# Splitting three of sixteen input tiles into 16 KiB row halves in a DMA-bound interleave

## The chip, the cores and the metric

One core of one Trainium2 chip. The metric is the device time of one execution in microseconds (us). In this document "before" and "after" are the two kernels, "x2" is the second x tile, "store 3" the third of the sixteen output stores, and "row" one partition's contiguous piece of a transfer, 32 KiB if nothing else is said.

## The reference

```python
batch, seq, dim = 32, 256, 1024          # x, y: float32, 33.55 MB each
result = np.zeros((batch, seq, dim * 2), dtype=np.float32)
result[..., 0::2] = x
result[..., 1::2] = y
```

Nothing is computed. 67.11 MB are read, 67.12 MB written.

## The kernel before: the parts that matter

Eight pairs of x and y tiles of 128 x 8192 elements (4 MiB) are loaded on one DMA queue (SP). Each pair gives two output tiles: VectorE (DVE) copies half of x to the even and half of y to the odd columns, and a second queue (ACT) stores 128 x 8192 elements. Each of these three pools has two buffers. A store of 8 KiB of zeros goes ahead of all others on the ACT queue, in both kernels; it explains the 0.01 MB more that are written.

```python
xpool = ctx.enter_context(tc.tile_pool(name="xp", bufs=2))   # yp, op: bufs=2 too
# ... cut ...
    nc.sync.dma_start(out=xtile, in_=xs)       # [128 x 8192], rows of 32 KiB
    nc.sync.dma_start(out=ytile, in_=ys)
    soff = 0
    while soff < lw:                           # two output tiles per pair
        # ... cut: otile and os_ ...
        nc.vector.tensor_copy(out=otile[:, 0::2], in_=xsub)
        nc.vector.tensor_copy(out=otile[:, 1::2], in_=ysub)
        nc.scalar.dma_start(out=os_, in_=otile)
        soff += width
```

So the two queues depend on each other: a store waits for an x and a y tile, a copy waits for the store two before it (its output buffer), a load waits for the copies of the pair two before it. Code that follows the loop moves the first load ahead of a barrier and shortens the end; the change leaves it alone.

## Time and profile before

| | before |
|---|---|
| median time, first measurement | 315.43 us (315.37 to 315.51) |
| span of the profiled run | 313.6 us |
| DVE busy | 72.8 us, 23% |

The lines of the page that carry this are in the prediction. One more view is needed later: the windows around the moment when the first store joins the loads, and one from the middle of the kernel to compare with. The columns are the stretch, its length, DVE busy time and count, POOL the same, clock, DMA share, and GB/s.

```profile
22.00:26.00 4.00, 4.00 (x2) 0.00 (x0) 1.00 0.95 410
26.00:30.00 4.00, 0.44 (x1) 0.00 (x0) 1.00 1.03 377
30.00:34.00 4.00, 0.00 (x0) 0.00 (x0) 1.00 1.02 442
...
182.00:186.00 4.00, 2.36 (x2) 0.00 (x0) 1.00 0.91 393
```

Read the last two columns together. A window of 4 us holds only some three rows of each engine, so GB/s alone swings, to 393 even in the middle of the kernel, but there the DMA share falls with it. GB/s divided by the share tells what the engines move while they are busy: 432, 366, 433 and 432 in these four windows. So there is a dent from 26 to 30 us, where the stores start: packets are in flight all along, at a share of 1.03, but last longer.

### The profile page before, as it was taken

Reading aid. Unit: us, or ns where it says so; the run is one execution under the profiler, and the core shown is the slowest. Engines: PE = TensorE matmul, PEld = TensorE weight load, DVE = VectorE, ACT = ScalarE, POOL = GpSimd, SP = SyncE. Lnnn points to the kernel's source line nnn. Section 1 sums busy time; section 2 is a strip of 40 time slices with the busy share of each in tenths; the row PEclk is TensorE's granted clock in tenths of the full one; section 3 lists DMA queues with packets and bytes.
Section 4 is the critical chain, followed back from the end, with each engine's and each line's share of the span. In section 5 each row is a group of like instructions: output and inputs, shape, how many; then the busy total and the mean of one; then the engine's idle time right before and its main releaser. Section 6 shows DMA issues by size and latency. Waiting matters only on the chain.

```text
span 313.6 us, 140 instructions
## 1 busy us (share of the span) xinstructions
DVE 72.8 (23%) x33; POOL 0.2 (0%) x4
## 2 busy tenths in 40 slices
DVE  0433002231022410325003150131501305023500
POOL 0000000000000000000000000000000000000000
DMA  8999999999999999999999999999999999999997
GB/s 344 460 405 397 464 405 464 405 464 405 460 410 447 422 439 431 435 435 426 443 410 460 401 468 401 468 401 464 405 464 405 464 405 460 410 447 422 439 431 334
DMA packets 4640, 134.23 MB, mean 428 GB/s; under 512 B 528, under 2 KB 544, under 8 KB 544
## 3 DMA queue, kind: packets, MB, share of 16 engines
q1 hardware_dynamic: 2304, 67.11, 50.0%
q10 hardware_dynamic: 2336, 67.12, 49.6%
HBM read 67.11 MB, written 67.12 MB: 428 GB/s over the span
## 4 chain that ended last, share of the span: by engine, by line
DMA 83%; DVE 11%; DVEq 1%; issue 0%
DMA out_dram<-otile 76%; DMA ytile<-in_y_dram 7%; DVE otile L72 6%; DVE otile L71 5%; DVEq L84 1%; DVEq L71 0%
## 5 line engine op out<-in xcount | busy, mean ns | idle before, releaser
L71 DVE COPY otile<-xtile 128x4096 f32<-128x4096 f32 x16 | 36.6, 2295 | 184.8 <-DMA out_dram<-otile 173.6
L72 DVE COPY otile<-ytile 128x4096 f32<-128x4096 f32 x16 | 36.6, 2292 | 39.8 <-DMA ytile<-in_y_dram 39.8
L46 DVE MEMSET zero<- 16x128 f32 x1 | 0.2, 165 | 0.9 <-PEq L134 0.9
L134 POOL MEMSET const-bfloat16-1.0<- 128x1 bf16 x1 | 0.1, 101 | 0.0
L134 POOL MEMSET const-uint8-127<- 128x1 uint8 x1 | 0.1, 101 | 0.0
L134 POOL MEMSET const-float32-0.0<- 128x1 f32 x1 | 0.1, 98 | 0.2 <-issue 0.2
L134 POOL MEMSET const-float32-1.0<- 128x1 f32 x1 | 0.1, 98 | 0.0
## 6 DMA issues: line engine op xcount, KB each, us to landing
out_dram<-otile ACTq DMA_DIRECT2D x16, 4096.0 KB, 29.1
xtile<-in_x_dram SPq DMA_DIRECT2D x8, 4096.0 KB, 43.6
ytile<-in_y_dram SPq DMA_DIRECT2D x8, 4096.0 KB, 60.7
out_dram<-zero ACTq DMA_DIRECT2D x1, 8.0 KB, 6.3
```

What stands on the lines that cost most here:

```text
L46: nc.vector.memset(zero, 0.0)
L71: nc.vector.tensor_copy(out=otile[:, 0::2], in_=xsub)
L72: nc.vector.tensor_copy(out=otile[:, 1::2], in_=ysub)
L84: tc.compile()
L134: nc = _bacc.Bacc("TRN2", target_bir_lowering=False, num_devices=1)
```

## The change

x2, y2 and y8 are loaded as two column halves, with rows of 16 KiB, so that copies can wait for half a tile and the stores get more of the engines beside those loads.

```diff
-        nc.sync.dma_start(out=xtile, in_=xs)
-        nc.sync.dma_start(out=ytile, in_=ys)
+        for t, s, parts in (
+            (xtile, xs, 2 if start == P * lw else 1),
+            (ytile, ys, 2 if start in (P * lw, total - P * lw) else 1),
+        ):
+            step = lw // parts
+            for c in range(0, lw, step):
+                nc.sync.dma_start(
+                    out=t[:, c : c + step],
+                    in_=dataclasses.replace(s, offset=start + c, ap=[[lw, P], [1, step]]),
+                )
```

## The prediction

> **What bounds the kernel now.** I read the page first: busy shares, the forty slices, the DMA queues. The columns of the slices are tenths of busy time, one digit per 7.84 us.
>
> ```profile
> DVE 72.8 (23%) x33; POOL 0.2 (0%) x4
> DMA  8999999999999999999999999999999999999997
> q1 hardware_dynamic: 2304, 67.11, 50.0%
> q10 hardware_dynamic: 2336, 67.12, 49.6%
> HBM read 67.11 MB, written 67.12 MB: 428 GB/s over the span
> ```
>
> The only compute engine with work, DVE, is busy 23%. The DMA engines are busy in every slice, and their two queues (q1 loads, q10 stores) fill 99.6% of 16 engines' span between them. A 4 MiB load has 128 rows; 16 loads of 128 rows plus 16 completion entries make 16 x 144 = 2304, the count of q1. So one packet is one 32 KiB row, and each of the 16 engines moves 8 rows of every tile.
>
> Second, the chain of waits. Read alone it misleads, and that is the trap here:
>
> ```profile
> by line: DMA out_dram<-otile 76.4%; DMA ytile<-in_y_dram 6.7%; DVE otile L72 5.7%; DVE otile L71 5.1%; DVEq L84 0.7%; issue 0.2%; DVEq L71 0.0%
> ```
>
> It says that the end waits on stores for 76% of the time, as if faster stores would shorten it. But a store takes long only because loads run beside it. Third, the queues' view of the stretch from 72 to 111 us shows this (columns: packets, MB, share):
>
> ```profile
> q1 hardware_dynamic: 288, 8.39, 49.8%
> q10 hardware_dynamic: 288, 8.39, 49.8%
> ```
>
> Equal packets and equal bytes: the engines serve the queues one row each in turn. Fourth, the timeline (start, length, instruction, idle before it and what ended it):
>
> ```profile
> 12.23 4.50 DVE L71 COPY otile<-xtile 128x4096 f32<-128x4096 f32 x2 [11.20 <-DMA xtile<-in_x_dram]
> 21.95 4.50 DVE L72 COPY otile<-ytile 128x4096 f32<-128x4096 f32 x2 [5.22 <-DMA ytile<-in_y_dram]
> 48.10 2.29 DVE L71 COPY otile<-xtile 128x4096 f32<-128x4096 f32 x1 [21.66 <-DMA out_dram<-otile]
> 55.31 2.29 DVE L72 COPY otile<-ytile 128x4096 f32<-128x4096 f32 x1 [4.92 <-DMA ytile<-in_y_dram]
> 67.47 2.29 DVE L71 COPY otile<-xtile 128x4096 f32<-128x4096 f32 x1 [9.87 <-DMA out_dram<-otile]
> 94.03 2.30 DVE L72 COPY otile<-ytile 128x4096 f32<-128x4096 f32 x1 [4.96 <-DMA ytile<-in_y_dram]
> 132.76 2.29 DVE L72 COPY otile<-ytile 128x4096 f32<-128x4096 f32 x1 [4.92 <-DMA ytile<-in_y_dram]
> 287.66 2.30 DVE L72 COPY otile<-ytile 128x4096 f32<-128x4096 f32 x1 [4.92 <-DMA ytile<-in_y_dram]
> 293.79 2.30 DVE L71 COPY otile<-xtile 128x4096 f32<-128x4096 f32 x1 [3.83 <-DMA out_dram<-otile]
> ```
>
> Loads alone: x1 lands at 12.23, y1 at 21.95, so 9.72 us for 8 rows, 1.215 us a row. With both queues: y3 lands at 94.03, y4 at 132.76, so 38.73 us for 32 rows an engine, 1.21 us a row or 2.42 us for a load row and a store row. The two rates agree to 0.4%. One queue with work fills the engines; a second only divides them. The whole work is 256 rows an engine, 256 x 1.21 = 309.8 us of a span of 313.6. Of the other 3.8 us, some 2.5 are the start (12.23 - 9.72); what is left is the last landing and the end of the program. **The bound is total DMA work, not stores.**
>
> **What the Trainium skill says.** "DMA: Bandwidth & Descriptors", section "Queues, rings and completion order": each DMA engine round-robins between the queue rows that have work, at packet granularity. The 288 against 288 packets above agrees. The same page, "Where 436 GB/s comes from": a ceiling of 435.2 GB/s, set by 16 ports. The trace's steady period moves 16.78 MB in 38.73 us, 433 GB/s, so it stands within 0.5% of it. The same page, "Why small descriptors are slow (HBM only)": a fixed overhead of about 3 cycles a packet; no run here isolates it yet. "SBUF — State Buffer", "The DMA setup-cost knee": a roughly fixed 2 us a transfer, mostly completion latency; the 2.5 us of x1 is of that kind, and behind a queued transfer it is hidden, since y1 came 9.72 us after x1.
>
> **The change part by part.** No byte is added or removed. The loads of x2, y2 and y8 become two each, of 16 KiB rows, so q1 gets 3 x 144 = 432 more packets. DVE and ACT keep their instructions in order. The built order shows that the copies wait on halves separately: the third pair of copies needs x2's and y2's first halves only, and the very last y copy alone needs y8's second half. It also shows one new wait in the load queue: y2's second half waits for x1's semaphore. That is over at 12.23 us, while y1 still loads, so it costs nothing.
>
> *Share.* Where 16 KiB load rows meet 32 KiB store rows in turn, a store row comes every 1.5 x 1.21 = 1.82 us in place of 2.42, and stores get two thirds of the engines. I carry this through. In before, x2 and y2 (16 rows) land 33.36 us after y1; n rows at 1.215 and 16 - n at 2.42 give n = 4.46 rows alone, then sharing from 27.4 us. Store 1 landed at 48.10, so in landing terms it began 8 x 2.42 earlier, at 28.7, which is 4.5 us after its issue.
> - Store 1 lands at 28.7 + 8 x 1.82 = 43.3 (48.10 before), store 2 at 57.8 (67.47).
> - Loads: 3.54 rows of x2 are left, 7.1 halves, then 8 halves of y2's first part: 27.4 + 15.1 x 1.82 = 54.8. After a copy of 2.29 store 3 is issued at 57.1 and begins, with the same 4.5 us, at 61.5. **So stores starve for 3.7 us.** Loads run alone then, y2's second half lands at about 62, and the engines stay full.
> - x3 starts at 62, not 55.3, and lands at about 81.3; store 3 lands at 80.3 (86.77 before), so the copy after it waits for x3. Store 4 ends at 99.7; y3 lands at 99.5 (94.03), store 5 begins at 101.8 + 4.5 = 106.3, a store gap of 6.6 us. In it x4 gets 4.5 rows alone, just as x2 did at the start, then 3.5 rows at 2.42 and y4's 8 give y4 at 132.9 against 132.76 before.
>
> The head start of the stores is thus handed back in full by about 125 us, with the engines busy all along: gain 0.
>
> *End.* x8 lands at 287.66 - 8 x 2.42 = 268.3. y8's first half takes 8 x 1.82, to 282.8, the second to 297.3 (whole y8 before: 287.66). Store 14 lands at about 292 (293.79 before). The last y copy ends at 297.3 + 2.3 = 299.6, and store 16 is issued then, against 298.3 before. Store 15 holds the engines till about 303.4 in landing terms (293.79 + 8 x 1.21), since the bytes ahead of it are the same. Store 16's entry needs 2.5 us (x1's, alone) to 4.5 us (store 1's, shared): ready at 302.1 to 304.1. The chance of a bubble is real, its size at most 0.7 us; near the lower figure there is none.
>
> *Packets.* 24 more rows an engine. Estimate from the skill's 27.2 GB/s an engine (435.2 / 16): a 32 KiB row would take 1.205 us, the trace has 1.210, so at most 0.006 us a row is overhead of any kind: 24 x 0.006 = 0.14 us, and three more completion entries of like size, 0.02 us.
>
> Sum: 315.43 + 0.16 + 0 for the shares + a bubble of 0 to 0.7 that I weight down to 0.05 = 315.6.
>
> **The rivals.**
> 1. *Stores are the bound, as the chain says.* Then 9.6 us earlier for store 2 would carry to the end: about 306 us. Against it: the DMA slices show no room, and 306 less the launch would ask for 134.23 MB in some 304 us, 441 GB/s, over every steady rate seen here. I give it almost nothing.
> 2. *A starved store queue becomes idle engines.* Loads fall 7 us behind, and with two buffers a tile each load waits on copies. If both queues ran dry in the two store gaps, up to 3.7 + 6.6 = 10.3 us would be lost: 326. Against it: x3 and y3 are issued at 16.75 and 26.5, long before they are needed, and by my count x4 at 60 and y4 at 64, ahead of the second gap.
> 3. *Half rows cost more per byte.* They are 12 MiB of 128, about 29 us of DMA time; 5% worse would be 1.5 us, 317. Nothing in the trace has 16 KiB rows, so this is not excluded.
> 4. *The bubble ahead of store 16*: up to 0.7 us, 316.3.
> 5. *Turns go by bytes, not packets*: no shift at all, 315.5. The trace before cannot tell, all rows being equal.
>
> **Range and chances.** 315.6, with 0.7 us below for a boundary or a start that I misplaced, and 1.0 above for rivals 3 and 4 in part: 314.9 to 316.6. Two per cent is 6.3 us, more than the 3.8 us not spent on rows, so faster has 0.01; slower needs rival 2, 0.02; within 2% 0.97.
>
> **What would show it.** Right: loads x19, q1 with 2736 packets; the third x copy starts near 43.3 and the fourth near 57.8; a new DVE wait for x3 ends near 81; y4 lands within 1 us of 132.8; the DMA row of the slices stays at 9; the last y copy starts near 297. With turns by bytes the third x copy stays near 48. Wrong: a slice with DMA at 7 or less in the middle, a y4 several us late, or a gap in DMA between the last two stores of over 1 us.

## The result, and the profile after

| | before | after |
|---|---|---|
| median | 315.47 us | 318.01 us |
| lowest to highest of 6 runs | 315.35 to 315.84 | 316.45 to 323.67 |
| ratio of the fast runs | | 1.006, interval 1.0035 to 1.0084 |

A ratio is the mean time of one kernel's fast runs over that of the other's in the same rounds, so it is not quite the ratio of the two medians. Two of the six runs of after (322.80 and 323.67) count as slow, being over 1.5% above the fastest run of their kernel, and are left out of it; no clock below 1.00 is on record for them, and no run of before was so far above its fastest. The change is a small loss, and it makes the time scatter: the four fast runs alone cover 1.9 us, where six of before cover 0.5.

The page of after, the lines that answer to those of the prediction:

```profile
DMA  9999999999999999999999999999999999999996
...
q1 hardware_dynamic: 2736, 67.11, 49.9%
q10 hardware_dynamic: 2336, 67.12, 49.3%
HBM read 67.11 MB, written 67.12 MB: 425 GB/s over the span
```

And the chain of waits of after, its shares by line:

```profile
by line: DMA out_dram<-otile 63.5%; another core or an unknown queue 11.9%; DMA ytile<-in_y_dram 6.8%; DVE otile L82 6.5%; DVE otile L81 5.8%; issue 0.9%; DVEq L81 0.1%
```

The 2736 packets are as counted, the DMA row still says 9, and the chain hangs on stores for 63.5% of the time where it was 76.4%. (Its "unknown queue" pieces, 11.9%, stand in the timeline of after at the waits for y2, x3, y3 and y8.) The page does not show where two microseconds went: they are lost inside slices that read "busy". The queues' view from 30 to 54 us of after, while half rows meet whole store rows:

```profile
q10 hardware_dynamic: 230, 7.01, 67.6%
q1 hardware_dynamic: 231, 3.28, 31.9%
```

Equal packets, twice the bytes for stores: turns go by rows, as predicted. The timeline of after:

```profile
45.12 2.29 DVE L81 COPY otile<-xtile 128x4096 f32<-128x4096 f32 x1 [18.41 <-DMA out_dram<-otile]
54.89 2.30 DVE L82 COPY otile<-ytile 128x4096 f32<-128x4096 f32 x1 [7.48 <-DMA ytile<-in_y_dram]
59.69 2.29 DVE L81 COPY otile<-xtile 128x4096 f32<-128x4096 f32 x1 [2.51 <-DMA out_dram<-otile]
...
64.63 2.29 DVE L82 COPY otile<-ytile 128x4096 f32<-128x4096 f32 x1 [2.64 <-DMA ytile<-in_y_dram]
...
84.02 2.29 DVE L81 COPY otile<-xtile 128x4096 f32<-128x4096 f32 x1 [17.09 <-DMA xtile<-in_x_dram]
...
133.95 2.30 DVE L82 COPY otile<-ytile 128x4096 f32<-128x4096 f32 x1 [4.37 <-DMA ytile<-in_y_dram]
...
299.35 2.29 DVE L82 COPY otile<-ytile 128x4096 f32<-128x4096 f32 x1 [3.12 <-DMA ytile<-in_y_dram]
```

Every event of the predicted ledger is there, in order, and each is 0.1 to 2.7 us late against it (43.3, 54.8, 57.8, 62, 81.3, 132.9, 297.3). The new wait for x3 ends at 84. The windows at the start of the stores, as above, now for after:

```profile
22.00:26.00 4.00, 3.79 (x2) 0.00 (x0) 1.00 1.00 430
26.00:30.00 4.00, 0.71 (x1) 0.00 (x0) 1.00 1.10 344
30.00:34.00 4.00, 0.00 (x0) 0.00 (x0) 1.00 0.98 422
```

The dent is deeper: GB/s over share is 430, 313 and 431, where before had 366 in the middle window.

**Looking at the sixteen engines one by one.** A transfer is complete when each of 16 DMA engines has set its mark. The Trainium skill says so in "DMA: Bandwidth & Descriptors", section "Why a DMA increments its semaphore by 16 and not by 1": the engines "finish independently, and the semaphore counts them". The trace has a time for each mark. First, middle (median) and last of the 16, worked out from those records:

```
                       before                      after
                       first   middle  last        first   middle  last
y1                     21.41   21.64   21.92       21.33   21.65   22.19
store 1                47.57   47.67   47.97       42.99   44.02   44.99
y2 (after: 2nd half)   54.84   54.97   55.29       61.20   62.83   64.61
x3                     74.21   74.34   74.65       80.88   82.20   83.94
y4                    132.29  132.42  132.74      131.49  133.08  133.92
y8 (after: 2nd half)  287.19  287.31  287.63      296.12  297.70  299.33
store 16              312.60  312.72  313.04      313.05  313.67  315.03
```

In before the sixteen marks of a transfer lie within 0.5 us for the whole kernel. In after they spread to 3.4 us and stay apart. Every wait is for the last of them. The end is later by 1.99 us (313.04 to 315.03). Of this the mean of the marks gives 0.99 (312.75 to 313.74), and the lag of the last behind the mean gives 1.00 (0.29 to 1.29). The other 0.26 of the 2.25 us by which the spans differ lies behind the last landing; I did not look into it.

The packets can be sorted into 16 chains, since on a busy engine one starts as the one before ends; each chain then holds 256 rows' worth of bytes, with a few packets put down to the wrong one in some of the runs. An engine's delay is its time less 1.2105 us for each row done. That gives a ledger for every run, shown after the experiments.

### The profile page after: what moved, and what is told of

It is laid out like the page before. It is cut to its first block, busy times and chain, and to the rows that moved or that the text cites. A ratio compares the mean times of both kernels' runs of the same rounds, so it can differ in the third digit from the quotient of the medians.

```text
span 315.8 us, 144 instructions
## 1 busy us (share of the span) xinstructions
DVE 72.9 (23%) x33; POOL 0.2 (0%) x4
## 3 DMA queue, kind: packets, MB, share of 16 engines
q1 hardware_dynamic: 2736, 67.11, 49.9%
## 4 chain that ended last, share of the span: by engine, by line
DMA 70%; DVE 12%; another core or an unknown queue 12%; issue 1%; DVEq 0%
DMA out_dram<-otile 63%; DMA ytile<-in_y_dram 7%; DVE otile L82 6%; DVE otile L81 6%; DVEq L81 0%
```

## The experiments

Thirteen runs were made, in four calls, before and after themselves among them; each call was on one chip (4, 6, 7 and 7), with before beside it. The first theories: A, the loss arises where stores first start beside half rows of x2; B, the shifted share costs in itself; C, each half row costs alike. After the first call came D: where the stores outrun the loads, restarts set the engines apart; against P: half rows cost by themselves. The edits of the loads are given as the two lines that choose `parts`, and all edits are written here more shortly than in the runs (there, for one, `start // (P * lw) in (1,)`), to the same effect. The intervals beside the ratios are 95%.

### First call: one part at a time

Only x2 halved:

```diff
-            (ytile, ys, 2 if start in (P * lw, total - P * lw) else 1),
+            (ytile, ys, 1),
```

> Only the second x tile is loaded in two halves. Theory A (the loss comes where stores first start beside 16 KiB load rows, near 26 us): nearly the whole loss, ratio 1.004 to 1.008, the 16 landings of the last store 1.5 to 2.5 us apart (0.45 before), and times that scatter by several us as in the changed kernel. Theory B (the loss comes from the shifted share and the starving store queue): about half the shift, so a ratio of 1.002 to 1.004. Theory C (every half row costs alike): a third of the loss, ratio 1.002, no scatter.

316.21 us (316.07 to 316.31), ratio 1.0015 (1.0003 to 1.0027). The delay at the start of the stores is there, 1.21 us against 0.66, but not the whole loss, and the times do not scatter. The last marks are only 0.18 us apart: store 15 was issued so late that the engines sat idle for 0.28 us on average, and all left that wait together. Theory A in its strong form is out.

Only y2 halved:

```diff
-            (xtile, xs, 2 if start == P * lw else 1),
-            (ytile, ys, 2 if start in (P * lw, total - P * lw) else 1),
+            (xtile, xs, 1),
+            (ytile, ys, 2 if start == P * lw else 1),
```

> Only the second y tile is loaded in two halves; stores now start beside 32 KiB rows of x2. Theory A: no loss, ratio 1.000 to 1.001, landings of the last store about 0.5 us apart, no scatter. Theory B: stores still get two thirds during y2, ratio 1.002 to 1.004. Theory C: ratio 1.002.

316.67 us (315.73 to 317.67), ratio 1.0032 (1.0015 to 1.0048). Here A expected nothing, while B's range holds it. In the profiled run the mean of the last marks is only 0.22 us later than before's; one engine is 0.85 us behind that mean.

Only y8 halved:

```diff
-            (xtile, xs, 2 if start == P * lw else 1),
-            (ytile, ys, 2 if start in (P * lw, total - P * lw) else 1),
+            (xtile, xs, 1),
+            (ytile, ys, 2 if start == total - P * lw else 1),
```

> Only the last y tile is loaded in two halves, far from the start of the stores. Theory A: ratio within 1.000 to 1.001, spread of the last landings about 0.5 us. Theory C: ratio 1.002. If a bubble ahead of the last store were the cause (the bubble of the prediction): ratio 1.002 to 1.005 and an idle stretch between the last two stores.

316.19 us (315.33 to 317.20), ratio 1.0016 (1.0002 to 1.0029). In the profiled run nearly all of the loss was in place at 32 us, 195 us before y8 is even issued: 0.92 us of delay at the start of the stores, three engines 2 us late in their stores. So this profile cannot charge the loss to y8's halves, and no idle stretch lies between the last two stores. What the halves of y8 themselves cost is not separated. Until 226 us this run issues what before issues, so 0.92 against 0.66 also shows how much that start differs between executions.

x2 and y2 halved, y8 whole:

```diff
-            (ytile, ys, 2 if start in (P * lw, total - P * lw) else 1),
+            (ytile, ys, 2 if start == P * lw else 1),
```

> Second x and y tile in halves, last y whole. Theory A: as x2 alone, ratio 1.004 to 1.008, scatter of several us. Theory B: the same. Theory C: two thirds, 1.004. If the halves of the last y tile matter, this is clearly faster than the changed kernel (1.006).

316.70 us (316.19 to 318.43), ratio 1.0042 (1.0023 to 1.0061). Not to be told from after's 1.006, nor from the sum of its two parts. By size alone, the ratios of the parts (1.0015, 1.0032, 1.0016) add up to after's, as theory C wants it; but C has no such price in the trace, as the next calls show.

### Second call: chance, place and dose

Before, unchanged, as a control:

> The kernel before, unchanged, as a control: how far one profile of it differs from another. If stepping out of line at the start of the stores is only chance and happens in it too, its engines' last landings are sometimes 1 us apart and its mean delay at that start 0.6 to 0.9 us; time 315.4 to 316.0, ratio 1.000.

315.74 us (315.45 to 316.00), ratio 0.9996 (0.9984 to 1.0008), on chip 6. Delay at the start of the stores 0.68 us, last marks 0.49 us apart. The order of before is no accident of one profile.

After, unchanged:

> The changed kernel, unchanged, on another chip: ratio 1.005 to 1.010, again times that scatter by 2 us or more, last landings 1 us or more apart and a delay of 1.1 to 1.3 us at the start of the stores (near 26 us). If the scatter was a matter of the first chip, all times lie within 1 us.

317.77 us (316.02 to 333.04; the highest counts as slow), ratio 1.0054 (1.0016 to 1.0093). The loss and the scatter came again, here on chip 6. In its profile y8's second half spread over 4.6 us, its last mark came at 300.54, and store 16 could only be issued then. Its windows near there:

```profile
296.00:302.00 6.00, 2.85 (x2) 0.00 (x0) 1.00 1.00 431
302.00:306.00 4.00, 0.86 (x1) 0.00 (x0) 1.00 0.86 369
```

This is the bubble of the prediction's rival 4: 0.41 us of idle time an engine, in this run, none in the other profile of after. The slowest engine decides whether it opens.

The fourth pair halved in place of the second:

```diff
-            (xtile, xs, 2 if start == P * lw else 1),
-            (ytile, ys, 2 if start in (P * lw, total - P * lw) else 1),
+            (xtile, xs, 2 if start == 3 * P * lw else 1),
+            (ytile, ys, 2 if start == 3 * P * lw else 1),
```

> The same halves two tile pairs later, in the fourth x and y tile, when stores have long run. Theory A (the loss is at the first meeting of stores and half rows): no more than 1.001 to 1.002. Theory D (any stretch with halves lets the store queue starve, and engines that are out of line then lose time at each restart): 1.003 to 1.005 like the second tile.

318.27 us (316.14 to 319.15), ratio 1.0068 (1.0041 to 1.0094). Theory A allowed 1.002 at most. The loss does not need the first start of the stores. In the profile 37 rows after 32 us last over 5% longer than they should, 0.85 us an engine, most of them near 160 and 183 to 186 us, long after the halves. And y8, whole here, lands between 287.98 and 292.43 us, one engine 4 us after the middle. The timeline and the windows of this run:

```profile
292.45 2.29 DVE L82 COPY otile<-ytile 128x4096 f32<-128x4096 f32 x1 [6.91 <-DMA ytile<-in_y_dram]
294.78 7.46 ACTq L83 DMA_DIRECT2D out_dram<-otile  x2
```

```profile
290.00:294.00 4.00, 1.55 (x1) 0.00 (x0) 1.00 0.91 393
294.00:298.00 4.00, 1.38 (x2) 0.00 (x0) 1.00 0.67 287
```

No loads are left, store 14 is done on most engines, and store 15 waits for the slowest engine's y8: a share of 0.67. That is 1.46 us of idle time an engine. Here GB/s over share stays at 432 and 428: engines that idle lower both, rows that last longer lower the quotient.

The same trace has a restart that the argument has to take in. From about 177 us the store queue runs dry again, and it restarts near 184 us with whole rows alone on both queues:

```profile
182.00:186.00 4.00, 3.47 (x2) 0.00 (x0) 1.00 1.05 393
```

The quotient is 374. By the packets, the last load row ahead of the first store row lasted 1.2 to 2.1 times its length on 11 of the 16 engines. The marks of y5, which landed just before, were 2.3 us apart. So a restart can cost without half rows beside it, in this run where the engines were already out of step.

x2 in four quarters, all else whole:

```diff
-            (xtile, xs, 2 if start == P * lw else 1),
-            (ytile, ys, 2 if start in (P * lw, total - P * lw) else 1),
+            (xtile, xs, 4 if start == P * lw else 1),
+            (ytile, ys, 1),
```

> Second x tile in four quarters with 8 KiB rows, all else whole. Theory A, with a dose: the delay at the start of the stores grows over the 1.2 us of halves (0.7 with whole rows), to some 1.5 us; if the delay is set by a fixed time in which loads run at half speed, it stays at 1.2 us. Store 1 should land near 41, as stores get four fifths while x2 loads.

316.21 us (315.93 to 316.42), ratio 1.0010 (0.9997 to 1.0023). The delay at the start is 1.22 us, as with halves (1.21): not a dose per row. Store 1's middle mark is at 41.3, as expected. The engines are 5.4 us apart near 60 us and back within 0.62 at the end: being apart for a while does not cost the end by itself.

### Third call: shares against rows

All loads halved, all stores whole:

```diff
-            (xtile, xs, 2 if start == P * lw else 1),
-            (ytile, ys, 2 if start in (P * lw, total - P * lw) else 1),
+            (xtile, xs, 2),
+            (ytile, ys, 2),
```

> All loads in two halves, all stores whole: stores get two thirds in every tile pair, so the store queue runs dry and restarts again and again. Theory D (each restart beside unequal rows sets engines further apart and the 16 landings are waited for together): well above the changed kernel, ratio 1.010 or more, last y landings 4 us or more apart. Theory P (half rows cost by themselves): 240 more rows an engine at the 0.002 us that a half row showed, and the start of the stores once, ratio 1.003 to 1.005 and no scatter.

321.69 us (321.44 to 321.80), ratio 1.0185 (1.0171 to 1.0200). The largest loss. (The 240 in the expectation is a slip: 4608 packets on q1 in place of 2304 are 128 more rows an engine, which makes theory P's share smaller still.) Marks of one transfer are up to 8.85 us apart, 135 rows are stretched (2.50 us an engine) and the engines idle for 1.77 us. Its list of who waits for whom has turned over; the first two lines (total us, times, longest), and then the line of before for the wait for y:

```profile
DVE otile L82 <- DMA ytile<-in_y_dram: 118.3, 16, 16.3
DVE otile L81 <- DMA out_dram<-otile: 101.3, 7, 14.9
```

```profile
DVE otile L72 <- DMA ytile<-in_y_dram: 39.8, 8, 5.2
```

So the wait for y grew from 39.8 to 118.3 us: the stores now outrun the loads, and each store is started by the slowest engine's load.

All loads and all stores halved, which adds to the edit just shown:

```diff
-            nc.scalar.dma_start(out=os_, in_=otile)
+            for c in range(0, 2 * width, width):
+                nc.scalar.dma_start(
+                    out=dataclasses.replace(
+                        of, offset=2 * start + 2 * soff + c, ap=[[2 * lw, P], [1, width]]
+                    ),
+                    in_=otile[:, c : c + width],
+                )
```

> All loads and all stores in halves: twice the rows, but the two queues take equal turns and the store queue does not run dry. Theory D: ratio 1.002 to 1.006 (some 1 us of row cost, 0.5 us at the start of the stores), landings of one transfer within 1.2 us of each other, scatter under 1 us. Theory P: more than all loads in halves, as it has twice as many half rows.

317.16 us (317.15 to 317.21), ratio 1.0044 (1.0032 to 1.0056). Twice as many half rows as in the run before, and 64 transfers in place of 48, with a quarter of its loss: theory P is out, and so is the number of transfers. The marks of a transfer lie 0.3 us apart through the middle of the run, one row is stretched, and the five times cover 0.06 us. The price of a row can be read here: from 32 to 288 us the mean delay grows by 1.08 us while before's falls by 0.07; 256 us are 211 rows of 1.2105, each cut in two, so 1.15 / 211 = 0.005 us an extra row.

All rows whole, x3 loaded ahead of y2, so that store 3 comes late and its queue runs dry (the kernel before, cut to the core of the edit):

```diff
+            if start == P * lw:          # second pair: its y waits behind the next x
+                ahead = load_x(2)        # the third pair then uses `ahead`
             nc.sync.dma_start(out=ytile, in_=ys)
```

> All rows whole; the third x tile is loaded ahead of the second y tile, so that the third store comes late, the store queue runs dry near 67 us for some 7 us and restarts, as in the changed kernel, but without half rows. If a restart by itself costs: 0.3 us or more of delay near 73 us, ratio 1.002 or more, engines out of line after it. If it takes half rows to set the engines apart: ratio 1.000 to 1.001, landings after the restart within 0.6 us, or as far apart as they were before it.

315.56 us (315.33 to 316.30), ratio 0.9996 (0.9983 to 1.0009). The timeline of this run shows the late store:

```profile
67.56 2.29 DVE L81 COPY otile<-xtile 128x4096 f32<-128x4096 f32 x1 [17.07 <-DMA out_dram<-otile]
...
71.14 4.50 DVE L82 COPY otile<-ytile 128x4096 f32<-128x4096 f32 x2 [1.28 <-DMA ytile<-in_y_dram]
73.47 2.56 ACTq L83 DMA_DIRECT2D out_dram<-otile  x2
```

Store 2 has landed at 67.5 and store 3 is issued at 73.5. The engines go on with loads, the delay does not move (2.65 us at 32 and at 60, 2.64 at 110), and the last marks are 0.48 us apart. The windows around the restart, near 78 us, have no dent (GB/s over share 434 and 431):

```profile
74.00:78.00 4.00, 1.64 (x1) 0.00 (x0) 1.00 1.04 451
78.00:82.00 4.00, 0.00 (x0) 0.00 (x0) 1.00 0.93 401
```

The expected 0.6 us between marks was missed: from 84 us until the loads end they are 1.2 to 1.7 us apart, since three engines took one load row more ahead of their first store row. That changed the order of turns and cost nothing. So in this run, with marks 0.5 us apart when it came, a dry and restarted store queue was free; loads did fill it, as I had predicted. With the fourth pair halved, where the engines were out of step, it was not (above).

x2 and y2 halved with the two stores beside them halved too (stores of the first pair only, same store edit under `start == 0`):

> Second x and y tile in halves, and the two stores of the first tile, which run beside them, in halves too: equal turns, no starved store queue, first y halves still allow an early third store. Theory D: mean delay at the start of the stores of 0.7 to 1.2 us, then flat; ratio 1.001 to 1.003, under the second tile's halves alone (1.004), with less scatter (under 1 us). If half rows and not shares set the engines apart: as the second tile's halves alone, 1.004.

316.31 us (316.03 to 316.76), ratio 1.0014 (1.0001 to 1.0027), against 1.0042 for the same loads beside whole stores. The delay at the start is 0.83 us in place of 1.27. The intervals just overlap, and the profile is not clean: its engines were 3.4 us apart at worst and 32 rows were stretched, 0.45 us an engine, after the stores had gone back to whole rows. So this supports D in the time but not in the order of the engines that I expected.

### Fourth call: the mirror

All stores halved, all loads whole: the loads edit of the kernel before with the store edit shown above.

> The mirror of all loads in halves: all stores in halves, all loads whole, so loads get two thirds of the turns in bytes. If unequal rows on the two queues set the engines apart whichever side is short: later rows stretched by 1 us an engine or more, landings of one transfer 3 us or more apart, ratio 1.008 or more. If it takes stores that outrun the loads (a store queue that runs dry and restarts beside short load rows): some 128 x 2 more rows at 0.005 us, ratio 1.003 to 1.005, landings within 1.5 us, few stretched rows.

316.37 us (316.13 to 316.53), ratio 1.0016 (1.0004 to 1.0029). No row after 32 us is stretched, no engine idles, marks stay within 1.81 us. That is the second case, though the ratio lies below its range and the marks above its 1.5 us (the edit adds 128 rows an engine, not 128 x 2; at 0.005 us they are 0.64 us). The same inequality the other way round costs 0.16%, where halved loads beside whole stores cost 1.85%. So it is not inequality as such: it takes short load rows beside long store rows. Stores that get ahead of the loads came with that in every run, so the two are not separated.

### The ledger of all runs

Worked out from the packets and the marks of each profiled run, in us. "Start" is the growth of the mean delay from 24 to 32 us, where the stores first join (not given where they join before 24); "stretched" counts the rows after 32 us that last over 5% longer than 1.213, 0.611 or 0.308 us for their size, with the excess for each engine; "idle" adds gaps of over 0.1 us on an engine after 32 us; "mean" is how much later than before's the mean mark of the last store lands; "last" is how far its last mark is behind that mean; "apart" is the widest spread of a transfer's marks after 30 us.

```
kernel                       ratio   start  stretched    idle   mean   last   apart
before                               0.66     0  0.00    0.00   0.00   0.29   0.46
before again                 0.9996  0.68     0  0.00    0.00   0.04   0.34   0.53
x3 ahead of y2, whole rows   0.9996  0.67     1  0.01    0.00   0.08   0.30   1.73
x2 in quarters               1.0010  1.22     0  0.00    0.00   0.67   0.38   5.37
second pair and its stores   1.0014  0.83    32  0.45    0.00   0.79   0.58   3.38
x2 halves                    1.0015  1.21     0  0.00    0.28   0.93   0.09   2.87
y8 halves                    1.0016  0.92     2  0.02    0.00   0.29   0.65   2.22
all stores in halves         1.0016  0.58     0  0.00    0.00   0.83   0.36   1.81
y2 halves                    1.0032  0.81     1  0.02    0.00   0.22   0.85   2.25
x2 and y2 halves             1.0042  1.27     0  0.00    0.00   0.69   0.47   3.07
all loads and stores         1.0044  -        1  0.02    0.02   1.44   0.62   0.86
after again                  1.0054  0.99    35  0.49    0.41   1.43   2.09   4.62
after                        1.006   1.23    30  0.27    0.00   0.99   1.29   3.41
x4 and y4 halves             1.0068  0.94    37  0.85    1.46   2.84   1.03   4.47
all loads in halves          1.0185  -      135  2.50    1.77   5.67   1.02   8.85
```

Ratios come from several runs, the other columns from one profile each. For after the mean of 0.99 is accounted for: 0.57 more at the start (1.23 - 0.66), 0.27 of stretched rows, and 24 more rows and 3 more completion entries at 0.005, 0.14; together 0.98. No version beats before.

## Why the prediction was wrong

The change stayed within 2%, as expected, but 318.01 lies above the range of 314.9 to 316.6.

**Right:** the bound. Store 2 landed ahead, 7.8 us in place of the predicted 9.6, and that did not carry to the end, so the chain of waits was rightly not believed (rival 1). Turns by rows, so rival 5 fell: 230 and 231 packets with 7.01 and 3.28 MB. The packet term, 0.16 us, against 0.14 worked out with 0.005 us a row. The order of events, the store gap near 60 us and the new wait for x3. No store gap left the engines idle (rival 2): the chains of after have no gap of over 0.1 us after 32 us. Rival 3, a dearer byte in half rows, is the 0.005 us a row and no more.

**Missed on the way:** y4. In the prediction's terms, the start of the copy that waits for it, it came at 133.95, where 132.9 was predicted and "within 1 us of 132.8" was to show it right. Against before its middle mark is 0.66 us later and its last 1.18. Two sums of that ledger also do not follow from the lines before them: 61.5 + 8 x 2.42 is 80.9 and not 80.3 for store 3, and 81.3 + 8 x 2.42 is 100.7 and not 99.5 for y3 (measured 101.05). And the 2.5 us of x1 are not of the kind that the prediction takes from the page on SBUF, mostly completion latency: in the packets of before 1.25 us pass on average until an engine's first row begins, that row takes 0.65 us longer than the later ones, and the mark follows the last row by 0.3 us.

**The step that failed:** "The head start of the stores is thus handed back in full by about 125 us, with the engines busy all along: gain 0." The 0 for the shares was the wrong term. It treats the sixteen engines as one. In the profiled run 0.84 us in the mean (0.57 and 0.27) and 1.00 us for the slowest engine stood in its place, two parts that "busy" hides:

- *Rows last longer, on busy engines.* Where the stores first join, load rows are stretched in both kernels. The mean delay of that is 0.66 us in before and 1.23 in after; across the runs it is 0.66 to 0.94 with whole x2 rows and whole stores, and 0.99 to 1.27 with short x2 rows. Later stretched rows add 0.27. I had taken the 33.36 us between y1 and y2 as rows at 1.215 and 2.42 alone, which buried the dent in the fitted row count of 4.46 and carried it over unchanged.
- *The end waits for the slowest of sixteen.* The last mark of store 16 was 0.29 us behind the mean and is 1.29. The prediction has one landing time for each transfer.

**The bubble:** I put store 16's bubble at 0 to 0.7 us with a weight of 0.05 in the sum. One profile of after has none, the other 0.41 us, so its size fits; whether 0.05 was too little, two profiles cannot say. That it depends on the slowest engine's y8 is seen with x4 and y4 halved, where the same kind of wait ahead of store 15 cost 1.46.

**Shown and not shown.** Shown by paired runs: short load rows beside whole stores cost up to 1.0185; the same loads beside short stores 1.0044; short stores beside whole loads 1.0016; a restart with whole rows nothing, when the engines were in step. That restarts are what costs (theory D) is not shown: in the first profile of after no load row ahead of the restarts near 60 and 107 us was stretched by over 5%; in the second one rows near 60 us were, on five engines. Argued only: why a row is stretched when the other queue's rows come in, and why that repeats on single engines in some executions; the trace has the length of a packet and not its reason. Not separated: what y8's halves add. Not profiled: the runs at 322.80, 323.67 and 333.04 us. The kernel with all loads halved shows that the same chain can cost some 6 us, but that those runs are the same thing is a guess. All of some fifty executions of before were under 316.6.

## What to carry to other kernels

When two DMA queues share saturated engines, giving one of them shorter rows moved turns to the other here and won nothing; if it lets the stores outrun the loads, it can also pull the sixteen engines apart, and every wait then costs the slowest one. Keep row lengths equal on both queues, and compare the first, middle and last completion mark of a transfer: a DMA row of nines cannot show this, but GB/s divided by the DMA share of a short window can show rows that last longer. For a change whose whole effect is under 1%, widen the predicted range by what a break in an orderly pattern could cost, not only by the terms that can be counted.

## What the Trainium skill lacked or had wrong

- "DMA: Bandwidth & Descriptors", "Queues, rings and completion order" has round-robin turns by packets, typically of some 9 to 17 descriptors. In these traces a recorded packet, and so a turn, is one row, of 16 or 32 KiB: 230 store packets against 231 load packets with 7.01 against 3.28 MB; how many descriptors a row has they do not show. The section does not say that row lengths therefore set the shares.
- The same page, "Why a DMA increments its semaphore by 16 and not by 1" says that the engines finish independently; no page says how far apart. Here: 0.5 us with equal rows in before, 3.4 us in after, 8.85 us with all loads halved.
- The same page, "Why small descriptors are slow (HBM only)" gives about 3 cycles a packet, and no time for rows of this size. Here an extra 16 KiB row cost 0.005 us (kernel with all loads and stores halved).
- No page has the dent where a store queue first joins a busy load queue: 0.66 us an engine in before, 1.23 us in after (GB/s over DMA share of 366 and 313 from 26 to 30 us, 430 to 433 on both sides of it).
- No page warns that short load rows beside long store rows cost more than short rows on both sides: ratios 1.0185 and 1.0044.
